# Small loads and stores on GpSimd's queue, a margin in the order of TensorE's work, and longer lines for the cache products

## The chip, the cores and the metric

The kernel runs on one core of one Trainium2 chip. The metric is device time in microseconds (us) of one launch, the median over runs. TensorE (PE in the profile; PEld is its weight load), VectorE (DVE), ScalarE (ACT), GpSimd (POOL) and SyncE (SP) each run their own instruction stream in order. Transfers between HBM and SBUF are issued from an engine's queue, and 16 DMA engines carry them.

## The reference

One layer of a hybrid decoder in float32, for 512 prompt tokens and for 8 sample tokens that have 4096 cached positions each:

```python
z = rmsnorm(x) @ w_in                      # 1024 -> 3584
o_hg, s_hg = hgrn2_recurrence(...)         # gated linear recurrence, 4 heads
o_da = attend(q_da, k_da, v_da, lam)       # differential attention, 4 heads, 2 maps each
x = x + concat(o_hg, o_da) @ w_out
x = x + cross_attn(rmsnorm(x), mk, mv)     # 256 memory tokens
x = x + swiglu(rmsnorm(x), w_gate, w_up, w_down)   # 1024 -> 2816 -> 1024
y = rmsnorm(x)
```

For the sample tokens the attention reads 8 x 32 pages of 128 positions of a key cache and as many of a value cache (67 MB each), found through a page table, and the recurrence makes one step from a stored state for each of the 8 requests. Outputs are y, the new states, and the new keys and values of both parts and of the memory.

## The kernel before

**Weights.** All weights are read once as a planned list of 512 KB pieces (`load_weights`, SP's queue, ring of 3 `raw` buffers). Each half piece (128x512, a "weight tile") is split by ACT (`hi`) and DVE (`lo`), and a product of the prompt is three matmuls on such splits. `done["used"]` counts the weight tiles consumed: w_in is 0 to 56, the memory's keys and values 56 to 88, w_out, w_mq and w_mo 88 to 136, and the feed-forward weights the rest.

**Cache.** Key pages and value pages come as 512 KB buffers (2 pages) of a ring of 6, also over SP's queue. `score_keys` consumes 128 such buffers in lumps of 4 (64 matmuls into `ks`); `sum_values` consumes 128 more (matmuls into `pv`). `pace` gives these streams a high rank as long as they are behind a straight line over the weight tiles, and a rank behind the prompt's products when they are ahead of it: `KPACE = (10, 62)` is the line for the keys, `VPACE = (60, 136)` that for the values.

**The sample recurrence** (`sample_recurrence`, once for the prompt's recurrence heads are under way): `svq` is written to a scratch in DRAM (`spill`, tile `vd`); then for each of 8 requests the state `st` (256 KB) is loaded, and `kv`, one row of `vd` spread over all 128 partitions in runs of 512 bytes (`load_row`, 256 KB). ACT multiplies `kv` by the key column, DVE updates `st`, `st` is stored as `hg_sample`, and TensorE forms `so` from it.

**The order of work** is written by a planner that runs while the program is built. `Clock` keeps an estimate of when each engine, tile and transfer is free; `note` adds each instruction as it is emitted. Every piece of work is a generator (a stream) with a rank. It yields a tuple of tiles ("when these are ready"), nothing ("when what I just issued is done"), a time, or a condition. `Weave.run` walks the streams by rank and lets the first go on whose time is not later than TensorE's estimated free time; if there is none, the one with the earliest time. The engines execute in the order in which the planner emitted, and wait on semaphores where the estimate was too early. The estimate for a transfer on SP's queue is: it begins 1.1 us after issue, moves 0.39 MB per us behind the transfers before it, and is known 0.93 us after its end.

All transfers but the load of the parameters and half of the final stores are on SP's queue.

Of the kernel before, what the change touches and what calls it, by code (L numbers as in the profile page):

```python
# [20 lines left out]
P = 128  # L21
# [12 lines left out]
LAM_INIT = 0.2  # L34
LEVELS = (16, 8, 4, 2, 1)
BIG = 1e37
SLOTS = 62
SCRATCH = 4
RAW = 3
HILO = 3  # L40
KPG = 2
KBUFS = 6
LUMP = 4
KPACE = (10, 62)
VPACE = (60, 136)
NEAR, FAR = 2, 4
PBATCH = 8
LEAD = 10.0
# [84 lines left out]
class Clock:  # L133
# [99 lines left out]
    def note(self, e, op, ins):  # L233
        i = ins.ins
        outs = [y.bass_ap for y in i.outs if hasattr(y, "bass_ap")]
        srcs = [y.bass_ap for y in i.ins if hasattr(y, "bass_ap")]
        mine = lambda aps: [a.tensor.name for a in aps if self.tc.is_my_tile(a.tensor)]
        ws, rs = mine(outs), mine(srcs)
        start = self.free[e]
        at = "dma" if op == "dma_start" else e  # L240
        for t in ws + rs:
            w, by = self.wrote.get(t, (0.0, ""))
            if by != at or at == "dma" and t in rs:
                start = max(start, w + self.LATE.get(by, 0.0))
        for t in ws if at != "dma" else ():
            start = max(start, self.used.get(t, 0.0))
        if op == "dma_start":
            start = max(start, self.free["issue"])
            self.free["issue"] = start + 0.56
            self.free[e] = start + (0.56 if e == "sp" else 0.06)  # L250
            begin = max(self.free["dma"], start + 1.1)
            a = outs[0] if ws else srcs[0]
            end = self.free["dma"] = begin + 4 * int(np.prod(a.shape)) / 0.39e6
            done = end + 0.93
            e = "dma"
        else:
            aps = outs + (srcs if e != "pe" else [])
            n = max(int(np.prod(a.shape[1:])) for a in aps)
            holds = self.shared(e, op, outs, srcs)
            if holds:  # L260
                for a, b in self.port["pool" if e == "dve" else "dve"]:
                    if a <= start < b:
                        start = b
            done = end = start + self._cost(e, op, outs[0].shape, [a.dtype for a in outs + srcs], n)
            if e == "pe":
                form = "narrow" if outs[0].shape[0] < P else "wide" if F32R in [a.dtype for a in srcs] else "exact"
                done = end = end + CHANGE.get((self.form, form), 0.0)
                self.form = form
                self.records += 2 if form == "wide" or op == "transpose" else 4
                if self.records >= 256:  # L270
                    self.records -= 256
                    done = end = self.fetched = max(end, self.fetched + FETCH)
                tick, rows = int(start / TICK), srcs[0].shape[0] / P
                if self.columns.get(tick - 1, 0) < FULL:
                    done = end = end + (end - start)
                self.columns[tick] = self.columns.get(tick, 0) + n * rows * (1 if F32R in [a.dtype for a in srcs] or op == "transpose" else 2)
            self.free[e] = end
            self.span = (start, end)
            if holds:
                self.port[e].append((start, end))  # L280
        for t in ws:
            self.wrote[t] = (done, e)
            self.mark = max(self.mark, done + self.LATE.get(e, 0.0))
        self.noted += 1
        for t in ws + rs:
            self.used[t] = max(self.used.get(t, 0.0), end)
            if t in self.banks:
                self.banks[t][1] = self.noted
# [19 lines left out]
class Weave:  # L308
# [8 lines left out]
        self.clock, self.streams = clock, []  # L317

    def add(self, gen, rank, uses=""):
        self.streams.append([rank, 0.0, None, gen, uses])  # L320

    @staticmethod
    def rank(s):
# [13 lines left out]
    def run(self):  # L337
        c = self.clock
        while self.streams:
            now = c.free["pe"]  # L340
            self.streams.sort(key=self.rank)
            best, when = None, 0.0
            for s in self.streams:
                if s[2] is not None:
                    if not s[2]():
                        continue
                    s[2] = None
                t = self._time(s)
                if best is None or t < when:
                    best, when = s, t  # L350
                if t <= now:
                    break
            assert best is not None, "every stream waits"
            c.mark = 0.0
            try:
                y = next(best[3])
            except StopIteration:
                self.streams.remove(best)
                continue
            if y is None:  # L360
                best[1] = c.mark
            elif callable(y):
                best[1], best[2] = 0.0, y
            elif isinstance(y, tuple):
                best[1] = c.ready(y)
            else:
                best[1] = y
# [3 lines left out]
def decode_step(ctx: ExitStack, tc: tile.TileContext, io: dict):  # L371
# [6 lines left out]
    pool = clock.engine("pool", real.gpsimd)  # L378
    sync = clock.engine("sp", real.sync)
# [5 lines left out]
    sp = ctx.enter_context(tc.tile_pool(name="sp", bufs=2))  # L385
# [175 lines left out]
    def spill(q, name):  # L561

        d = dp.tile([P, P], F32, name=name)
        sync.dma_start(d, q)
        return d.rearrange("(g b) c -> b g c", b=32)

    def load_row(dst, d, b):

        sync.dma_start(dst.rearrange("p (g c) -> p g c", g=4), d[b].partition_broadcast(P))


    sizes = [512] * (DFF // 512)
# [162 lines left out]
    S = {}  # L735
# [104 lines left out]
    def evac_qk(which):  # L840
        def f(t, acc):
            z = slot("z")
            act.activation(z, acc, AF.Copy, scale=rtok[:, t : t + 1])
            return rotate(t, z)

        def rotate(t, z):
            yield (z,)
            yield from room()
            o = slot("ro")
            rope_tok(v3(z), ropep[:, t, :], v3(o))  # L850
            yield (o,)
            if which == "k":
                sync.dma_start(io["k_prompt"][t * P : (t + 1) * P, :], o)
            yield from at_room()
            pt = att("qkt")
            for h in range(HEADS):
                tr(pt[:, h * P : (h + 1) * P], o[:, h * P : (h + 1) * P], ident)
            yield (pt,)
            if which == "q":
                qT[t] = slot("qT")  # L860
                act.copy(qT[t], pt)
                give(1)
            else:
                for h in range(HEADS):
                    if kT[h] is None:
                        kT[h] = slot("kT")
                    act.copy(kT[h][:, t * P : (t + 1) * P], pt[:, h * P : (h + 1) * P])
                give(2)
                done["k"] += 1
            at_give()  # L870

        return f
# [6 lines left out]

    def store(dst, t):  # L880
        yield (t,)
        sync.dma_start(dst, t)

    def s_rope(acc, scale, name, read=None):
        z = quadt("sz", tag="fq", bufs=3)
# [97 lines left out]
    def score_keys():  # L983

        yield lambda: "qst" in S
        for n in range(0, NB * nst, LUMP):
# [4 lines left out]
            yield lambda: n + LUMP - 1 in kts  # L991
            yield (*(kts[n + i] for i in range(LUMP)), *qst)
            cols = slice(s % 4 * P, (s % 4 + 1) * P)
            for y in range(2):
                for b in range(b0, b0 + LUMP):
                    for g in range(4):
                        h = 2 * (g % 2) + y
                        mm(
                            acc[32 * g : 32 * g + 32, cols],
                            qst[b // 4][:, b % 4, h, :],  # L1000
                            kts[n + b - b0][:, g // 2, h * P : (h + 1) * P],
                            b + y == 0,
                            b + y == NB,
                        )
# [301 lines left out]
    def hg_head(h):  # L1306
# [104 lines left out]
            )  # L1411
        at_give()
        yield
        sync.dma_start(io["hg_prompt"][h], st[:, 3 * P :])
        yield from at_room()
        out = att("ohg")
        for c in range(NT):
# [48 lines left out]
    def sample_recurrence(sqT, sfT, svq, sgT):  # L1466
# [14 lines left out]
        yield from room(2)  # L1481
        for b in range(NB):
            st = slot("st")
            sync.dma_start(st, io["state"][b])
            kv = slot("kv")
            load_row(kv, vd, b)
            yield
# [14 lines left out]
                    st[:, sl], st[:, sl], sfT[:, h, b : b + 1], kv[:, sl], op0=ALU.mult, op1=ALU.add  # L1502
                )
            yield
            sync.dma_start(io["hg_sample"][b], st)
            yield from at_room()
            po = att("so")
            for h in range(HEADS):
# [79 lines left out]
    def evac_mk(half):  # L1588
# [4 lines left out]

        def rest(t, o):
            yield (o,)
            sync.dma_start(io["mem_k"][t * P : (t + 1) * P, half * 512 : (half + 1) * 512], o)
            yield from at_room()
            pt = att("mkt")
            for j in range(4):
# [39 lines left out]
    def load_residual():  # L1639
        for j in range(KT):  # L1640
            yield from room()
            xr[j] = slot("res")
            sync.dma_start(xr[j], io["xpT"][j * P : (j + 1) * P, :])
            yield 0.0

    def squares(t, sq):
# [440 lines left out]
    def sample_query(hs):  # L2087
# [16 lines left out]
        yield from s_gemm(hs, 2560, acc[:, :P], KT, width=P)  # L2104
        yield (acc,)
        S["k"] = yield from s_rope(acc[:, :P], 1.0, "ks", at_give)
        sync.dma_start(io["k_sample"], S["k"])
        yield from new_scores()
        S["sn"] = True
        yield lambda: V_FROM in raws  # L2110
# [494 lines left out]
```

## Time and profile before

| | |
|---|---|
| median of 3 runs | 1150.04 us (1149.22 to 1154.39) |
| the profiled execution, its own time | 1160.71 us |
| its span, first to last instruction | 1158.6 us |
| mean granted TensorE clock | 0.974 of full speed |
| busy: PE, PEld, DVE, ACT, POOL | 94%, 68%, 48%, 37%, 3% |
| moved by DMA | 271.38 MB, mean 234 GB/s |

The profiled execution is one run of the program under the hardware profiler; its stages and waits are read by their size against its own time, and the runs without profiler are the metric. A busy PE is not a PE at its peak: the ends of matmuls are modelled. A granted clock of 1.00 in a stretch means 2.4 GHz throughout, and the part that is missing was run at 1.2 GHz.

### The profile page before, as it was taken

What the parts mean: (1) busy time and instruction counts of PE and PEld (TensorE: products, weight loads), DVE (VectorE), ACT (ScalarE), POOL (GpSimd) and SP (SyncE); (2) the same over time, 40 slices, a digit from 0 to 9 for tenths busy, and PEclk for the clock granted to TensorE, in tenths of its full rate; (3) what the DMA queues carried; (4) which work ended last, traced back from release to release, by engine and by line L of the source; (5) the groups of instructions that cost most, each with busy time, mean ns of one, the idle gap of its engine ahead of it and who ended that gap; (6) DMA issues with size and microseconds to landing.
All of it is one profiled execution on the core that took longest, in us unless ns stands there. A gap on an engine that the chain in (4) does not pass through costs nothing.

```text
span 1158.6 us, 23172 instructions
## 1 busy us (share of the span) xinstructions
PE 1092.8 (94%) x8909; PEld 783.3 (68%) x8909; DVE 551.9 (48%) x1128; ACT 427.8 (37%) x910; POOL 38.5 (3%) x42
## 2 busy tenths in 40 slices
PE   8999899978778899999999999999999999999997
PEld 6767677755556544666677766556678788777776
DVE  6741787513655654244355544333334335344545
ACT  5411544313635665233354423223123122222333
POOL 0000010000400000000011000000000000000001
PEclk9999999989888899999999999999999999999998
DMA  7889958878888689999987687999843221233202
GB/s 263 297 296 308 308 197 277 294 256 244 282 257 291 186 300 353 358 366 327 331 264 253 202 309 268 372 366 378 287 154 87 87 83 52 68 109 110 56 1 73
DMA packets 146273, 271.38 MB, mean 234 GB/s; under 512 B 14833, under 2 KB 25073, under 8 KB 146162
## 3 DMA queue, kind: packets, MB, share of 16 engines
q1 hardware_dynamic: 144930, 268.79, 68.1%
q8 instruction: 70, 1.15, 0.4%
q10 hardware_dynamic: 1232, 1.11, 0.3%
q14 instruction: 41, 0.34, 0.1%
HBM read 260.96 MB, written 8.88 MB: 233 GB/s over the span
## 4 chain that ended last, share of the span: by engine, by line
PE 71%; DMA 16%; DVE 5%; SPq 3%; issue 3%; ACT 2%; DVEq 0%; ACTq 0%
PE mm L301 49%; DMA cache_k<-cache_k 6%; PE pv L301 5%; PE ks L301 4%; SPq L301 3%; DMA cache_v<-cache_v 2%; DMA kv<-vd 2%; PE cs L301 2%; PE sdn L301 2%; PE sgu L301 2%; DMA raw<-w_in 1%; PE sgm L301 1%; DMA gu<-w_up 1%; PE co L301 1%; DVE lo L301 1%
## 5 line engine op out<-in xcount | busy, mean ns | idle before, releaser
L301 DVE TENSOR_TENSOR lo<-raw,hi 128x512 fp32r<-128x512 f32 (+1 forms) x260 | 177.5, 684 | 414.2 <-ACT hi L301 362.9
L301 PE MATMUL mm<-sh,hi 128*128 128x512 f32 (+1 forms) x832 | 339.3, 408 | 0.3 <-ACT hi L301 0.3
L301 ACT CAST hi<-raw 128x512 fp32r<-128x512 f32 (+1 forms) x260 | 157.3, 606 | 460.0 <-PE mm L301 407.1
L301 PE MATMUL mm<-sl,hi 128*128 128x512 f32 (+1 forms) x832 | 323.9, 389 | 0.6 <-DVE sl L301 0.6
L301 PE MATMUL mm<-sh,lo 128*128 128x512 f32 (+1 forms) x832 | 323.1, 388 | 0.0
L301 PEld LDWEIGHTS mm<-sh,hi 128*128 128x128 f32 x832 | 157.5, 189 | 73.5 <-issue 39.0
L301 PEld LDWEIGHTS mm<-sh,lo 128*128 128x128 f32 x832 | 157.6, 189 | 33.7 <-DVE lo L301 0.4
L301 PEld LDWEIGHTS mm<-sl,hi 128*128 128x128 f32 x832 | 158.0, 190 | 28.4 <-DVE sl L301 1.0
L301 PE MATMUL ks<-cache_k,qst 128*32 128x128 f32 x2048 | 78.3, 289 | 9.1 <-DMA cache_k<-cache_k 7.7
L301 PEld LDWEIGHTS ks<-cache_k,qst 128*32 128x32 f32 x2048 | 59.8, 115 | 29.8 <-DMA cache_k<-cache_k 19.9
L301 PE MATMUL pv<-cache_v,wt 128*32 128x512 f32 x512 | 67.6, 599 | 1.2 <-DMA cache_v<-cache_v 1.2
L301 PE MATMUL mm<-hi,sh 128*128 128x512 f32 x128 | 56.2, 439 | 0.0
L301 PE MATMUL mm<-lo,sh 128*128 128x512 f32 x128 | 51.3, 401 | 0.0
L301 PE MATMUL mm<-hi,sl 128*128 128x512 f32 x128 | 51.2, 400 | 0.0
L301 DVE TENSOR_TENSOR res<-mm,res 128x512 f32<-128x512 f32 (+1 forms) x68 | 42.4, 654 | 11.4 <-PE mm L301 11.3
L301 PEld LDWEIGHTS pv<-cache_v,wt 128*32 128x32 f32 x512 | 15.2, 109 | 36.4 <-issue 22.5
L301 PEld LDWEIGHTS mm<-hi,sh 128*128 128x128 f32 x128 | 24.9, 195 | 7.9 <-issue 3.4
L301 PE MATMUL mm<-hi,mh 128*128 128x512 f32 x64 | 29.7, 464 | 0.0
L301 PEld LDWEIGHTS mm<-hi,sl 128*128 128x128 f32 x128 | 24.8, 194 | 5.8
L301 PEld LDWEIGHTS mm<-lo,sh 128*128 128x128 f32 x128 | 25.1, 196 | 4.5 <-issue 0.5
L301 PE MATMUL mm<-lo,mh 128*128 128x512 f32 x64 | 25.5, 399 | 0.0
L301 PE MATMUL mm<-hi,ml 128*128 128x512 f32 x64 | 25.5, 398 | 0.0
(410 smaller groups left out, 1170.3 us busy)
## 6 DMA issues: line engine op xcount, KB each, us to landing
cache_k<-cache_k SPq DMA_DIRECT2D x256, 256.0 KB, 5.5
cache_v<-cache_v SPq DMA_DIRECT2D x256, 256.0 KB, 5.0
raw<-w_in SPq DMA_DIRECT2D x27, 512.0 KB, 5.7
raw<-w_down SPq DMA_DIRECT2D x22, 512.0 KB, 3.8
raw<-w_gate SPq DMA_DIRECT2D x20, 512.0 KB, 4.1
raw<-w_up SPq DMA_DIRECT2D x20, 512.0 KB, 3.8
cache_mem_k<-cache_mem_k SPq DMA_DIRECT2D x16, 512.0 KB, 7.4
cache_mem_v<-cache_mem_v SPq DMA_DIRECT2D x16, 512.0 KB, 7.2
```

What stands on the lines that cost most here:

```text
L301: ins = getattr(self.engine, op)(*a, **k)
```

## The change

1. Transfers that are stores or small loads go from SP's queue to GpSimd's: `spill` (1), `load_row` (8), the stores of the prompt's keys (4) and values (4), of the sample's key and value (2), of the prompt's states (4), of the memory's keys (4) and values (4), the loads (8) and stores (8) of the sample's states, and the loads of the residual (8): 55 transfers. Weights, cache pages, x and the last stores stay where they were.
2. The planner's estimate for a transfer on GpSimd's queue: the queue is held 1.0 us, the transfer begins 2.0 us after issue. All transfers are estimated at 0.37 in place of 0.39 MB per us.
3. After a stream yielded a tuple of tiles or nothing, it counts as ready for the walk by rank only when TensorE's estimated time is `MARGIN = 1.0` us past its own. If no stream is ready with its margin, the one with the earliest time goes on, without a margin.
4. `KPACE` goes from (10, 62) to (10, 80), `VPACE` from (60, 136) to (80, 150), `SLOTS` from 62 to 63.
5. In `score_keys` the loop over the 4 buffers of a lump is put outside the loop over the two maps.

```diff
-SLOTS = 62
+SLOTS = 63
-KPACE = (10, 62)
-VPACE = (60, 136)
+MARGIN = 1.0
+KPACE = (10, 80)
+VPACE = (80, 150)
@@ Clock.note
         if op == "dma_start":
-            start = max(start, self.free["issue"])
-            self.free["issue"] = start + 0.56
-            self.free[e] = start + (0.56 if e == "sp" else 0.06)
-            begin = max(self.free["dma"], start + 1.1)
+            if e == "pool":
+                self.free[e] = start + 1.0
+            else:
+                start = max(start, self.free["issue"])
+                self.free["issue"] = start + 0.56
+                self.free[e] = start + (0.56 if e == "sp" else 0.06)
+            begin = max(self.free["dma"], start + (1.1 if e != "pool" else 2.0))
             a = outs[0] if ws else srcs[0]
-            end = self.free["dma"] = begin + 4 * int(np.prod(a.shape)) / 0.39e6
+            end = self.free["dma"] = begin + 4 * int(np.prod(a.shape)) / 0.37e6
@@ Weave.run
-                if t <= now:
+                if t + s[5] <= now:
+                    best = s
                     break
...
             c.mark = 0.0
+            best[5] = 0.0
...
+            if y is None or isinstance(y, tuple):
+                best[5] = MARGIN
@@ spill, load_row, evac_qk, store, hg_head, sample_recurrence, evac_mk, load_residual, sample_query
-        sync.dma_start(d, q)
+        pool.dma_start(d, q)
...
-        sync.dma_start(dst.rearrange("p (g c) -> p g c", g=4), d[b].partition_broadcast(P))
+        pool.dma_start(dst.rearrange("p (g c) -> p g c", g=4), d[b].partition_broadcast(P))
...
@@ score_keys
-            for y in range(2):
-                for b in range(b0, b0 + LUMP):
+            for b in range(b0, b0 + LUMP):
+                for y in range(2):
```

## Rows read from the trace of the kernel before

**Rows 1.** The page: span, and busy time of each engine.
```profile
span 1158.6 us, 23172 instructions
PE 1092.8 (94%) x8909; PEld 783.3 (68%) x8909; DVE 551.9 (48%) x1128; ACT 427.8 (37%) x910; POOL 38.5 (3%) x42
```
**Rows 2.** By stage: us, busy time of each engine, granted clock, DMA share, GB/s.
```profile
0.00:230.00 230.00, 213.62 (x3168) 165.94 (x3169) 139.28 (x312) 91.89 (x200) 8.98 (x15) 0.97 0.82 279
230.00:410.00 180.00, 146.97 (x1360) 103.59 (x1359) 88.58 (x229) 82.26 (x208) 12.34 (x9) 0.89 0.78 248
410.00:460.00 50.00, 45.44 (x280) 24.04 (x279) 24.85 (x58) 31.39 (x73) 0.00 (x0) 1.00 0.98 349
460.00:685.00 225.00, 225.00 (x1239) 148.42 (x1241) 95.71 (x168) 87.80 (x181) 11.30 (x10) 1.00 0.87 301
685.00:850.00 165.00, 163.67 (x1084) 103.57 (x1077) 64.10 (x129) 46.55 (x88) 0.62 (x2) 1.00 0.86 320
850.00:1096.00 246.00, 244.14 (x1507) 191.53 (x1506) 106.12 (x176) 67.59 (x124) 0.00 (x0) 1.00 0.30 90
1096.00:1158.60 62.60, 53.98 (x284) 46.20 (x282) 33.26 (x59) 20.32 (x38) 5.31 (x6) 0.95 0.11 35
```
**Rows 3.** Waits of all engines: engine, for what, us in total, times, longest.
```profile
ACT kv L301 <- DMA kv<-vd: 39.1, 7, 12.8
```
**Rows 4.** Timeline, PE and one row of ACT, 236 to 396: start, us, idle before it.
```profile
252.53 1.41 PE L301 MATMUL so<-st,qm 128*32 128x128 f32 x8 [5.76 <-issue]
...
267.42 1.28 PE L301 MATMUL so<-st,qm 128*32 128x128 f32 x8 [1.60 <-DVE st L301]
...
346.00 1.28 ACT L301 ACTIVATE kv<-kv,skT 128x128 f32<-128x128 f32 x4 [7.30 <-DMA kv<-vd]
...
347.67 0.79 PE L301 MATMUL sc<-kT,qT 64*128 64x128 f32 x2 [6.34 <-ACT pr L301]
...
371.49 1.12 PE L301 MATMUL mkt<-con,mk 128*128 128x128 f32 x4 [3.54 <-ACT mk L301]
...
395.87 1.65 PE L301 MATMUL oda<-pr,vda 128*128 128x128 f32 x6 [2.77 <-ACT pr L301]
```
**Rows 5.** The chain that ended last, in order of time: start, us, what.
```profile
258.96 1.88 PE ks L301 x64
...
348.46 3.57 PE ks L301 x64
```
**Rows 6.** Cache pages: idle before their products (us, times), the products, PE's own idle.
```profile
  DMA cache_k<-cache_k: 27.6, 57
...
  DMA cache_v<-cache_v: 14.3, 29
...
L301 PE MATMUL ks<-cache_k,qst x2048: 272/273/423, 51.7 to 376.8; 128*32 128x128 f32 x187
...
L301 PE MATMUL pv<-cache_v,wt x512: 592/592/617, 407.1 to 685.5; 128*32 128x512 f32 x171
...
L301 PE MATMUL ks<-cache_k,qst 128*32 128x128 f32 x2048 | 78.3, 289 | 9.1 <-DMA cache_k<-cache_k 7.7
...
L301 PE MATMUL pv<-cache_v,wt 128*32 128x512 f32 x512 | 67.6, 599 | 1.2 <-DMA cache_v<-cache_v 1.2
```
**Rows 7.** DMA issues: KB each, median us from issue to landing.
```profile
st<-state SPq DMA_DIRECT2D x8, 256.0 KB, 5.3
kv<-vd SPq DMA_DIRECT2D x8, 256.0 KB, 10.1
```
**Rows 8.** Waits of SP's queue, 230 to 300 and 300 to 420.
```profile
SPq L301 <- DMA vd<-svq: 4.1, 1, 4.1
...
SPq L301 <- DVE st L301: 9.5, 2, 9.1
```
**Rows 9.** POOL's costliest group, and DVE's (min/median/max ns).
```profile
L301 POOL TENSOR_TENSOR res<-sh,sl 128x512 f32<-128x512 f32 x8 | 10.5, 1342 | 287.5 <-ACT cp L301 281.1 <-PE co L301 6.4
...
L301 DVE TENSOR_TENSOR lo<-raw,hi x260: 422/692/1776, 5.9 to 1139.2; 128x512 fp32r<-128x512 f32 x122, 128x256 fp32r<-128x256 f32 x8
```

More of the change, by code (lines that the diff above doesn't have):

```diff
@@ L319, in add @@
     def add(self, gen, rank, uses=""):
-        self.streams.append([rank, 0.0, None, gen, uses])
+        self.streams.append([rank, 0.0, None, gen, uses, 0.0])
     @staticmethod
@@ L852, in rotate @@
             if which == "k":
-                sync.dma_start(io["k_prompt"][t * P : (t + 1) * P, :], o)
+                pool.dma_start(io["k_prompt"][t * P : (t + 1) * P, :], o)
             yield from at_room()
@@ L881, in store @@
         yield (t,)
-        sync.dma_start(dst, t)
+        pool.dma_start(dst, t)
     def s_rope(acc, scale, name, read=None):
@@ L1413, in hg_head @@
         yield
-        sync.dma_start(io["hg_prompt"][h], st[:, 3 * P :])
+        pool.dma_start(io["hg_prompt"][h], st[:, 3 * P :])
         yield from at_room()
@@ L1483, in sample_recurrence @@
             st = slot("st")
-            sync.dma_start(st, io["state"][b])
+            pool.dma_start(st, io["state"][b])
             kv = slot("kv")
@@ L1504, in sample_recurrence @@
             yield
-            sync.dma_start(io["hg_sample"][b], st)
+            pool.dma_start(io["hg_sample"][b], st)
             yield from at_room()
@@ L1595, in rest @@
             yield (o,)
-            sync.dma_start(io["mem_k"][t * P : (t + 1) * P, half * 512 : (half + 1) * 512], o)
+            pool.dma_start(io["mem_k"][t * P : (t + 1) * P, half * 512 : (half + 1) * 512], o)
             yield from at_room()
@@ L1642, in load_residual @@
             xr[j] = slot("res")
-            sync.dma_start(xr[j], io["xpT"][j * P : (j + 1) * P, :])
+            pool.dma_start(xr[j], io["xpT"][j * P : (j + 1) * P, :])
             yield 0.0
@@ L2106, in sample_query @@
         S["k"] = yield from s_rope(acc[:, :P], 1.0, "ks", at_give)
-        sync.dma_start(io["k_sample"], S["k"])
+        pool.dma_start(io["k_sample"], S["k"])
         yield from new_scores()
```

## Prediction

> **What bounds the kernel now.** I read the page first: TensorE is busy 94% of the span [rows 1], so a change that removes no product can win only what TensorE loses: its idle time and the time at the lower clock. The view by stages says where these lie [rows 2]. Up to 460 us TensorE idles 16.4 + 33.0 + 4.6 = 54.0 us; after that, 0 + 1.3 + 1.9 + 8.6 = 11.8 us, most of it in the last 63 us, which no part of the change touches. The granted clock is 0.97, 0.89 and 1.00 in the first three stages. A clock of 0.89 over 180 us costs 0.11 x 180 = 19.8 us of full-speed work, 0.97 over 230 us costs 6.9 us. So some 81 us are to be had before 460 us, and 53 of them in the 180 us from 230 to 410. The DMA engines are not full there (share 0.78), though they are from 410 to 460 (0.98 at 349 GB/s).
>
> What stalls TensorE between 230 and 410? The waits of the engines [rows 3] show ACT standing 39.1 us in 7 waits for the load of kv. ACT works in order, so the splits of weights and the softmax pieces emitted behind that multiply stand as well. The timeline shows the stalls that follow: 5.76 and 1.60 us before so, 6.34 before a score, 3.54 before a transpose, 2.77 before an attention product, together 20.0 us; the third ends 1.7 us after a kv wait of 7.30 us [rows 4]. The chain of waits then shows what a stall does to the clock [rows 5]: 64 key products take 1.88 us at full speed and 3.57 us right after the 6.34 us stall, the lower of the two levels (1.2 against 2.4 GHz). Kv takes so long because of its shape: it lands 10.1 us after issue, the state load of the same size 5.3 us [rows 7], while the planner reckons 1.1 + 0.67 + 0.93 = 2.7 us when the DMA queue is free.
>
> The second loss is spread out: before products on cache pages TensorE or its weight load sat 27.6 us in 57 waits for keys and 14.3 us in 29 waits for values; TensorE's own idle of it is 7.7 + 1.2 = 8.9 us [rows 6]. The third is SP's queue: in the stage of the recurrence it stood 9.5 us for a store that waited for DVE, and 4.1 us for the spill to land before kv could be issued [rows 8], with cache pages and weights queued behind.
>
> **The change, part by part.**
>
> *kv and its margin.* By the new estimate kv is due 2.0 + 0.71 + 0.93 = 3.64 us after issue, and the stream that yielded nothing gets 1.0 us more while others have work. ACT's multiply is therefore ordered 4.64 - 2.70 = 1.94 us later against the rest. If kv lands as late as now, 7 waits of 5.6 us on average shorten by 1.94 each: 13.6 of 39.1 us, or 35%. What hangs on these waits is 20.0 us of stalls and the stage's 19.8 us of clock, 39.8 us, about 1.0 us of TensorE per us of ACT's wait. The term is 0.35 x 39.8 = 13.9 us. Bounds: no row shows a transfer on GpSimd's queue. If kv lands like the state load, at 5.3 us, the waits vanish (5.3 - 4.64 is under 1 us) and the term is 39.8 us. If its shape costs as much again (10.1 - 5.3 = 4.8 us), it lands at 14.9 us and 8 loads lose 8 x 4.8 = 38 us. I take 10.1, the only row of this shape.
>
> *Margin, slower transfers, pace and loop order, for the cache products.* The mean wait there is 41.9 / 86 = 0.49 us, under the margin of 1.0. A 256 KB page is estimated 0.04 us longer, a lump of 8 pages 0.3 us. With the loop turned round the last buffer of a lump is first needed after 24 products, not 12: at 1.88 / 64 = 0.029 us each that is 0.35 us later. The key pace now spreads the last (80 - 62) / 70 = 26% of 67 MB, some 17 MB or 49 us of transfer at 349 GB/s, behind weight tile 62; the values follow by 14 tiles. That relieves the stages before 410 us and loads those from 410 to 850, where the DMA share is already 0.98 to 0.86 and TensorE has no idle time to lose it in. Nothing in all this moves more bytes per second, so part of what a product no longer waits for is waited for elsewhere. Bounds: 0, if all of it is, and 41.9 us. I take the row nearest to TensorE's own loss, 8.9 us.
>
> *SP's queue.* 9.5 + 4.1 = 13.6 us of standing go. What was late behind it were pages and weights; in this stage TensorE idles 33.0 of 180 us (18%), in the rest it had other work. 0.18 x 13.6 = 2.5 us; bounds 0 and 13.6. The store, and the next state load behind it, now stand on POOL's queue in the same order. What else is queued there is the gating of the recurrence heads, which w_out needs only from 460 us on, and later the residual's sums.
>
> *What GpSimd pays.* POOL is busy 38.5 us of 1158.6 [rows 1]. Even at the length of its longest common instruction, 1.342 us [rows 9], 55 issues are 74 us in an engine that idles 97% of the time: 0 on the path. SP sheds 55 issues; 0 too, since it waits for buffers anyway. The slot more is 0, nothing waits for slots in the rows read.
>
> *Later sample work.* The values end at tile 150 instead of 136. They took 278 us for the 76 tiles of their old line [rows 6], 3.7 us a tile, so the sample's remaining path starts some 51 us later. It moves into the stages from 685 to 1096, where TensorE is busy throughout and the DMA share falls to 0.30 [rows 2]: 0, covered by the feed-forward products, and up to 51 us if that path became the last to end.
>
> Sum: 13.9 + 8.9 + 2.5 = 25.3 us. The profiled execution would go from 1160.7 to 1135.4 us. It lies 10.7 us over the median of the runs, so I take the same 25 us from the median: 1150 - 25 = 1125 us.
>
> **A rule that speaks against it.** SP's queue, on which kv comes now, is held up by waits alone [rows 8]; no engine that computes takes part in it. The Trainium skill, "SBUF — State Buffer", section "SBUF: two separate sides", says that descriptors of transfers issued from GpSimd are written by GpSimd itself, which cannot write them while DVE holds their shared SBUF port in certain modes; its example goes from about 620 ns to about 3100 ns. By that example, an estimate, 8 loads of kv would lose 8 x 2.5 = 20 us, and the sum would be 5 us in place of 25. No row here shows a transfer on that queue, so the trace can't say yet.
>
> **Rivals.**
>
> *Slower: kv late on the new queue.* Its 512 runs are prepared by an engine that shares work time with DVE, which is busy 88.6 of 180 us in this stage [rows 2] in pieces of 0.69 us, up to 1.78 [rows 9]. Each us of later landing costs 8 us on ACT and, by the ratio above, 8 us on TensorE, so 25 / 8 = 3.1 us per load eat the gain, and the 4.8 us of the bound give 1125 + 38 = 1163 us. Against it: POOL is idle and its instructions finish beside DVE at 1.3 us.
>
> *More: kv quick on its own queue.* Now kv stands behind the pages issued before it on SP's queue. If a queue of its own lands it near 5.3 us, the first term is 39.8 instead of 13.9: 1125 - 26 = 1099 us. Against it: the state load stands on the same queue and needs half the time, so most of the 10.1 is the shape.
>
> *Nothing: the waits move.* The planner's order is as wrong as before elsewhere, the pages that come later stall the values from 410 to 850, where rows show the DMA engines full, and only SP's 2.5 us remain: 1147 us. For it: bytes and products are the same. Against it: the clock stage has its own cause, kv.
>
> **How the numbers follow.** Forecast (1110 to 1140): 0.48. More: 0.16. Nothing: 0.16. Slower: 0.20. A measurement of this kernel can tell about 0.5%, 5.8 us, from no change. Forecast and "more" are faster, with a sliver of "nothing" (0.01): 0.65. Same: 0.15. Slower: 0.20. The range goes from 1097, the "more" case, to 1158, which takes in "nothing" and the mild half of "slower"; outside it are about 0.06 below and 0.12 above.
>
> **What would show it.** Right: ACT's wait for kv falls from 39.1 to about 25 us; TensorE's idle time between the start of the recurrence and the end of the keys falls by some 10 us or more and the clock there rises over 0.92; the waits before cache products go well under 41.9 us; the keys end near weight tile 80 and the stages after that stay without idle time. Kv's landing decides between the cases: about 10 us for the forecast, 5 to 7 for more, 13 and over for slower. Wrong: ACT's kv waits as long or longer, POOL's transfers late, TensorE idle between 410 and 850 us, or the last stage waiting for the sample's path.

## The result, and the profile after

The changed kernel takes 1141.7 us (median of 6, 1134.9 to 1143.8) against 1152.2 us for the kernel before in the same comparison (1149.2 to 1157.5): ratio 0.9891, 95% interval 0.9849 to 0.9934. That is 10.5 us faster, where 25 us were forecast. The time lies inside the range and the direction holds; the gain is less than half of the forecast.

The two profiled executions differ by more than the medians: 1160.7 us before, 8.5 over its median, and 1134.9 after, 6.9 under its own. Of the 25.9 us between them 15.4 are not in the medians. The stages of the changed kernel, from its page and the view by stages (columns as in [rows 2]):

```profile
span 1133.1 us, 23098 instructions
...
PE 1072.3 (95%) x8846; PEld 777.3 (69%) x8846; DVE 546.1 (48%) x1126; ACT 428.3 (38%) x915; POOL 70.4 (6%) x97
...
0.00:230.00 230.00, 213.91 (x3025) 170.84 (x3026) 141.24 (x323) 93.42 (x207) 18.28 (x32) 0.96 0.77 255
230.00:410.00 180.00, 149.92 (x1468) 106.14 (x1470) 94.73 (x230) 90.27 (x224) 28.46 (x35) 0.92 0.96 284
410.00:460.00 50.00, 48.46 (x352) 34.51 (x341) 23.30 (x62) 30.20 (x68) 6.01 (x12) 0.98 0.71 238
460.00:685.00 225.00, 222.18 (x1248) 144.88 (x1249) 99.14 (x175) 88.24 (x180) 11.29 (x10) 0.99 0.91 311
```

Against [rows 2], the bad stage is still there: from 230 to 410 us TensorE idles 30.1 us (33.0 before) and the clock is 0.92 (0.89). The view of the waits says that its old cause has shrunk, ACT's waits for kv from 39.1 us [rows 3] to this:

```profile
ACT kv L305 <- DMA kv<-vd: 21.1, 3, 9.3
```

and the views of the cache pages' tiles say what came instead (idle before the products; key products first and last start; landing; then the values):

```profile
  DMA cache_k<-cache_k: 40.0, 36
...
L305 PE MATMUL ks<-cache_k,qst x2048: 272/273/423, 47.5 to 418.8; 128*32 128x128 f32 x187
...
DMA to landing us min/median/max: 2.7/5.6/15.4
...
  DMA cache_v<-cache_v: 8.3, 24
```

The waits for values fell from 14.3 to 8.3 us, those for keys rose from 27.6 to 40.0 [rows 6], in fewer and longer pieces. The key stage ends at 419 us instead of 377. TensorE's own waits from 230 to 410 us show the exchange, before and after: what it loses to the softmax and the recurrence shrinks, what it loses to key pages grows from 5.9 to 16.0 us.

```profile
PE sc L301 <- ACT pr L301: 6.3, 1, 6.3
PE ks L301 <- DMA cache_k<-cache_k: 5.9, 11, 2.1
PE so L301 <- issue: 5.8, 1, 5.8
```
```profile
PE ks L305 <- DMA cache_k<-cache_k: 16.0, 10, 6.0
PE sc L305 <- ACT pr L305: 4.9, 1, 4.9
PE so L305 <- issue: 3.6, 1, 3.6
```

The timeline of TensorE has the longest such wait, and the chain of waits what it waited for: a key page that was 13.7 us on its way; the store of a state, the load of a state and a kv were issued 0.9 to 2.0 us after it.

```profile
265.04 1.53 PE L305 MATMUL ks<-cache_k,qst 128*32 128x128 f32 x16 [5.99 <-DMA cache_k<-cache_k]
```
```profile
251.28 13.71 DMA cache_k<-cache_k
265.04 1.53 PE ks L305 x16
```

On GpSimd's queue kv lands after 11.4 us (10.1 before, [rows 7]), and an issue costs POOL 0.55 us, or 0.76 us for kv. The load of a quarter of the memory, which is still on SP's queue, lands after 12.5 us, where it took 9.4 before (DMA issues, then POOL's groups):

```profile
mt<-memT SPq DMA_DIRECT2D x4, 256.0 KB, 12.5
...
st<-state POOLq DMA_DIRECT2D x8, 256.0 KB, 6.1
kv<-vd POOLq DMA_DIRECT2D x8, 256.0 KB, 11.4
```
```profile
L305 POOL DMA_DIRECT2D kv<-vd x8 | 6.1, 758 | 5.4 <-DMA vd<-svq 5.4
...
L305 POOL DMA_DIRECT2D out_hg_sample<-st x8 | 4.4, 550 | 126.3 <-DVE st L305 78.4 <-DVE pz L305 22.8 <-DMA cache_k<-cache_k 14.5
```

### The profile page after: what moved, and what is told of

The parts are those of the page before. It is cut to its first block, busy times and chain, and to the rows that moved or that the text cites. A ratio compares the mean times of both kernels' runs of the same rounds, so it can differ in the third digit from the quotient of the medians.

```text
span 1133.1 us, 23098 instructions
## 1 busy us (share of the span) xinstructions
PE 1072.3 (95%) x8846; PEld 777.3 (69%) x8846; DVE 546.1 (48%) x1126; ACT 428.3 (38%) x915; POOL 70.4 (6%) x97
## 2 busy tenths in 40 slices
DMA packets 143376, 279.75 MB, mean 247 GB/s; under 512 B 15281, under 2 KB 20529, under 8 KB 143266
## 3 DMA queue, kind: packets, MB, share of 16 engines
q0 software_dynamic: 4064, 13.05, 6.1%
## 4 chain that ended last, share of the span: by engine, by line
PE 81%; DMA 10%; DVE 3%; issue 3%; ACT 1%; SPq 1%; POOL 0%; DVEq 0%; POOLq 0%; ACTq 0%
PE mm L305 56%; DMA cache_k<-cache_k 6%; PE pv L305 5%; PE ks L305 4%; PE sgu L305 2%; PE cs L305 2%; PE sdn L305 1%; DMA kv<-vd 1%; PE ss L305 1%; PE co L305 1%; PE sgm L305 1%; PE pd L305 1%; PE sacc L305 1%; PE oda L305 1%; PE cpv L305 1%
## 5 line engine op out<-in xcount | busy, mean ns | idle before, releaser
L305 PE MATMUL ks<-cache_k,qst 128*32 128x128 f32 x2048 | 72.3, 285 | 16.1 <-DMA cache_k<-cache_k 16.0
L305 PE MATMUL pv<-cache_v,wt 128*32 128x512 f32 x512 | 63.4, 608 | 0.0
L305 DVE SCALAR_TENSOR_TENSOR lo<-raw,par,hi 128x512 fp32r<-128x512 f32 x16 | 13.2, 826 | 35.1 <-ACT hi L305 35.1
L305 PE MATMUL mm<-hi,mh 128*128 128x512 f32 x64 | 28.5, 446 | 0.9 <-ACT hi L305 0.9
```

Of the source, the lines that this page charges most:

```text
L305: ins = getattr(self.engine, op)(*a, **k)
```

## The experiments

The kernel before had medians of 1149.1 to 1152.2 us in the comparisons below; each ratio is against it.

| kernel | median us | ratio, 95% interval |
|---|---|---|
| changed | 1141.7 | 0.989 (0.985 to 0.993) |
| e1 queue alone | 1167.1 | 1.015 (1.013 to 1.017) |
| e2 margin alone | 1142.9 | 0.992 (0.990 to 0.995) |
| e3 paces alone | 1150.5 | 1.001 (0.999 to 1.003) |
| e4 changed, kv a plain load | 1096.1 | 0.953 (0.951 to 0.955) |
| e5 changed, no margin | 1143.1 | 0.993 (0.989 to 0.996) |
| e6 changed, old paces | 1122.3 | 0.975 (0.972 to 0.978) |
| e7 changed, SP's queue | 1138.1 | 0.988 (0.983 to 0.993) |
| e8 changed, kv in 2 KB runs | 1098.2 | 0.955 (0.951 to 0.960) |
| e9 as e8, old paces | 1098.4 | 0.953 (0.950 to 0.957) |
| e10 as e8, no margin | 1112.8 | 0.966 (0.963 to 0.969) |
| e11 as e8, SP's queue | 1099.8 | 0.955 (0.952 to 0.959) |
| e12 before, kv in 2 KB runs | 1121.7 | 0.973 (0.969 to 0.976) |
| e13 changed, old key line | 1121.0 | 0.976 (0.972 to 0.979) |
| e14 changed, old value line | 1137.1 | 0.989 (0.986 to 0.991) |
| e15 changed, lines half way | 1148.2 | 0.999 (0.997 to 1.001) |
| e16 as e8, margin 2.0 | 1101.8 | 0.957 (0.955 to 0.960) |

**One part alone.** e1 takes part 1, in all ten calls, and of part 2 the estimate for GpSimd's queue:

```diff
-        sync.dma_start(d, q)
+        pool.dma_start(d, q)
...
+            if e == "pool":
+                self.free[e] = start + 1.0
```

> The kernel before with the 55 transfers on GpSimd's queue and their estimate alone; no margin, old paces, old loop order, 62 slots, 0.39 MB per us. Theory order (the gain is the margin's: it orders ACT's multiply by kv later): within 4 us of before, ACT's waits for kv still above 30 us. Theory queue (the gain is SP's queue freed of stores and spill): 6 to 12 us faster. Theory paces: within 4 us.

It is 18 us slower, so neither theory foresaw it. ACT's waits for kv nearly vanish, yet cache pages are late by far more (waits of the engines, then idle before key and value products):

```profile
ACT kv L305 <- DMA kv<-vd: 6.5, 2, 5.3
```
```profile
  DMA cache_k<-cache_k: 62.1, 63
...
  DMA cache_v<-cache_v: 36.3, 40
```

e2 takes part 3 alone:

```diff
+MARGIN = 1.0
...
-                if t <= now:
+                if t + s[5] <= now:
+                    best = s
                     break
```

> The kernel before with the margin of 1.0 us alone, all transfers on SP's queue. Theory order: 6 to 12 us faster, ACT's waits for kv about 30 us. Theory queue: within 4 us. Theory paces: within 4 us.

It is 6 us faster at the medians, as theory order said, but not for its reason: ACT's waits for kv stay at 41.1 us (39.1 before), while the waits before key products go from 27.6 to 21.6.

e3 takes the two lines of part 4 alone:

```diff
-KPACE = (10, 62)
-VPACE = (60, 136)
+KPACE = (10, 80)
+VPACE = (80, 150)
```

> The kernel before with the two longer lines for keys and values alone. Theory paces (fewer pages early relieve the first 410 us): 6 to 12 us faster, waits before cache products under 30 us. Theories order and queue: within 4 us, the waits only move.

No difference. The three parts add to a loss of some 13 us, and the change is a gain of 10. Either the parts do not add, or what was not run alone (loop order, 0.37, the slot) makes up 24 us; the next runs speak for the first.

**What kv does to the pages beside it.** e4 and e8 change one load of the changed kernel; e4 first.

```diff
-        pool.dma_start(dst.rearrange("p (g c) -> p g c", g=4), d[b].partition_broadcast(P))
+        pool.dma_start(dst, io["state"][b])
```

> The changed kernel in which each kv is loaded as a plain 256 KB state (128 rows of 2 KB) in place of one row spread over all partitions in runs of 512 bytes, so that the sample's recurrence is computed from other numbers; size, queue and order are the same. Theory shape (kv's pattern holds up the cache pages in flight beside it, which is where the gain went): kv lands in 5 to 7 us, the 40.0 us of waits before key products fall under 25, and the kernel is 8 to 20 us faster than the changed one. Theory full engines (the pages are late because the DMA engines are full then): kv lands at 9 us or later, the key waits stay above 33 us, and the time stays within 4 us of the changed kernel's.

And e8:

```diff
-        d = dp.tile([P, P], F32, name=name)
-        pool.dma_start(d, q)
-        return d.rearrange("(g b) c -> b g c", b=32)
+        d = dp.tile([32, T], F32, name=name)
+        for g in range(4):
+            pool.dma_start(d[:, g * P : (g + 1) * P], q[32 * g : 32 * g + 32, :])
+        return d
...
-        pool.dma_start(dst.rearrange("p (g c) -> p g c", g=4), d[b].partition_broadcast(P))
+        pool.dma_start(dst, d[b].partition_broadcast(P))
```

> The changed kernel with the scratch in DRAM written so that the row of a request lies in one piece of 2 KB (4 small transfers in place of one); each kv is then still one row spread over 128 partitions, but in 128 runs of 2 KB in place of 512 of 512 bytes. Theory runs (the number of short runs costs the time): kv lands in 5 to 8 us, the kernel is 20 to 45 us faster than the changed one. Theory one place (all 16 DMA engines read the same 2 KB of HBM, whatever the length of the runs): kv lands at 9 us or later and the time stays within 6 us of the changed kernel's.

They are 46 and 44 us faster than the changed kernel, and e8 does all its work. For e4 that is over twice what theory shape expected; its signs, kv's landing and the waits before key products, came as it said. The stage from 230 to 410, kv's landing, and the idle time before key products, first e4, then e8:

```profile
230.00:410.00 180.00, 172.85 (x1726) 126.24 (x1719) 111.99 (x275) 113.66 (x277) 30.12 (x44) 0.98 0.90 320
...
kv<-state POOLq DMA_DIRECT2D x8, 256.0 KB, 6.2
...
  DMA cache_k<-cache_k: 11.4, 22
```
```profile
230.00:410.00 180.00, 173.58 (x1739) 127.77 (x1741) 113.00 (x283) 113.94 (x278) 33.39 (x47) 0.99 0.92 323
...
kv<-vd POOLq DMA_DIRECT2D x8, 256.0 KB, 7.2
...
  DMA cache_k<-cache_k: 13.4, 25
```

TensorE idles 6.4 us in that stage in place of 30.1, the clock is 0.99 in place of 0.92, and the same DMA engines move 323 GB/s in place of 284, at a share of 0.92 in place of 0.96. So they were not full of bytes before: they were busy with kv. The page's line for GpSimd's queue shows it directly, the changed kernel first, then e8 (packets, MB, share of the 16 engines' span):

```profile
q0 software_dynamic: 4064, 13.05, 6.1%
```
```profile
q0 software_dynamic: 4160, 13.05, 3.4%
```

The same 13.05 MB took the 16 engines 6.1% of 1133.1 = 69 us and 3.4% of 1097.0 = 37 us, so the eight slow loads held all of them for 32 us more, 4.0 us each. Theory full engines falls, and so does theory one place, as 128 reads of one 2 KB row are quick. Whether it is the number of runs (512 against 128) or that a request's four pieces lay 16 KB apart in the scratch, the runs don't separate.

**The changed kernel with one part taken back.** e5 sets `MARGIN = 0.0`, e6 the two old lines, e7 puts `sync` for `pool` in all ten calls.

> The changed kernel with the margin set to 0. The queue alone made the kernel 18 us slower than before and the margin alone 7 us faster. Theory sum (the parts add): about 1149 us, 7 to 8 us over the changed kernel. Theory pair (the margin mends the damage of the queue's move, so without it the changed kernel falls back further): 1158 us or more, ACT's waits for kv above 30 us.

> The changed kernel with the old paces (10, 62) and (60, 136). Theory sum: within 4 us of the changed kernel, as the paces alone did nothing. Theory pair (the longer lines matter only beside the other parts, where more pages are in flight beside the slow kv): 6 us slower or more, waits before key products over 40 us.

> The changed kernel with all transfers back on SP's queue; margin, paces, loop order, slot and 0.37 stay. Theory sum: the queue's move costs 18 us, so this gives about 1124 us. Theory pair (the move pays once the margin orders the waits): 1141 us or slower.

Without the margin the changed kernel is 1.4 us slower, inside the scatter: neither theory. ACT's waits for kv are then 6.6 us, less than the 21.1 with it. On SP's queue it is 3.6 us faster at the medians, inside the scatter: under the 1141 of theory pair, but far from the 1124 of theory sum, as the 18 us of e1 are not there. ACT waits longer for kv in it than in the kernel before (39.1 us):

```profile
ACT kv L305 <- DMA kv<-vd: 48.5, 7, 9.8
```

The large one is e6: the longer lines cost 19 us here, though alone they cost nothing. Neither theory foresaw that sign. ACT waits 3.9 us for kv and key products 34.1 (waits; then the stage; then the tile):

```profile
ACT kv L305 <- DMA kv<-vd: 3.9, 4, 1.6
...
230.00:410.00 180.00, 161.77 (x1486) 117.08 (x1474) 103.32 (x266) 99.06 (x253) 29.99 (x39) 0.94 0.95 278
...
  DMA cache_k<-cache_k: 34.1, 37
```

**Which line, and is it steady?** e13 and e14 put back one line each, e15 sets (10, 71) and (70, 143).

> The changed kernel with the old line for the keys (10, 62) and the new one for the values. Theory overlap (longer key loading keeps pages in flight beside all eight slow kv loads): 1119 to 1127 us, as with both old lines. Theory values (the values' line costs it): 1138 us or more.

> The changed kernel with the old line for the values (60, 136) and the new one for the keys. Theory overlap: within 5 us of the changed kernel's 1142. Theory values: 1119 to 1127 us.

> The changed kernel with both lines half way, (10, 71) and (70, 143). Theory overlap: half way between, 1128 to 1136 us. Theory accident of order (small shifts decide what stands behind a slow kv): outside 1120 to 1143, or at one of the two ends within 3 us.

The keys' line costs nearly all of it: 1121.0 with the old one, while the old line for the values gives 1137.1, near the changed kernel's 1141.7. But half way is slower than either end, at 1148.2, with 28.5 us of ACT's waits for kv and 59.7 us before key products. So it does not grow with the line: theory overlap holds for which line, and theory accident for how much.

**The parts again, with a quick kv.**

> The changed kernel with kv in runs of 2 KB and with the old paces. In the changed kernel the new paces cost 19 us. Theory kv (they cost it because more of the key stage runs beside the slow kv): with the quick kv the difference shrinks, 1092 to 1104 us against 1098 with the new paces. Theory paces (the longer lines are bad by themselves): 1086 us or less.

> The changed kernel with kv in runs of 2 KB and the margin set to 0. Theory margin (products wait for results whose time is estimated too early, everywhere): 1104 us or more against 1098. Theory kv (what the margin did for the kernel before was to wait less behind kv): within 4 us of 1098.

> The changed kernel with kv in runs of 2 KB and all transfers back on SP's queue. Theory queue (stores that wait at the head of SP's queue hold up pages whatever kv does): 1104 us or more against 1098. Theory kv: within 4 us.

> The kernel before with nothing changed but kv in runs of 2 KB (and its scratch written in 4 pieces). Theory kv: 30 us or more faster than before, 1120 us or less, ACT's waits for kv under 12 us. Theory parts (the gain of the quick kv needs the margin and the queue): 1130 us or more.

> The changed kernel with kv in runs of 2 KB and a margin of 2.0 us. A margin of 1.0 gave 14.7 us with the quick kv. Theory more (estimates are off by more than 1 us in many places): 1092 us or less. Theory enough (1.0 covers the usual error): within 4 us of 1098.

Old paces 1098.4 and SP's queue 1099.8 against 1098.2: with a quick kv, and beside the margin, both parts are worth nothing that can be told from 0. The margin is worth 14.7 us (e10), so it does mend waits elsewhere: theory margin, not theory kv. The view of the waits shows some of the places, e10 first and e8 second (TensorE's own waits for DVE and the pauses of its weight load that no view puts down to another engine):

```profile
PE kdt L305 <- DVE zf L305: 5.0, 3, 2.5
PE pt L305 <- DVE pr L305: 4.0, 6, 1.6
...
PEld mm L305 <- issue: 56.1, 143, 0.8
```
```profile
PE kdt L305 <- DVE zf L305: 2.2, 1, 2.2
...
PE pt L305 <- DVE pr L305: 0.5, 1, 0.5
...
PEld mm L305 <- issue: 46.0, 114, 1.4
```

A margin of 2.0 gives 1101.8, no more than 1.0 does. The kernel before with nothing but the quick kv takes 1121.7 us, 29.7 under before, between the two theories (1120 and 1130); its stage from 230 to 410 idles 10.4 us:

```profile
ACT kv L301 <- DMA kv<-vd: 6.4, 4, 2.7
...
230.00:410.00 180.00, 169.56 (x1571) 113.47 (x1570) 106.94 (x281) 107.59 (x272) 11.27 (x9) 0.99 0.90 315
```

## Why the prediction was right in direction and wrong in size

**Where the loss lies** was right. The quick kv alone recovers 29.7 us of the kernel before, and the quick kv with the change 54: the stage and the load at its root were named.

**The premise** that the change can win only idle time and lost clock, with products and bytes the same, did not hold. Between the two profiled executions TensorE's idle time fell from 65.8 to 60.8 us and the mean clock is 0.974 in both, but its busy time fell from 1092.8 to 1072.3. The new order takes more of the sample's later weights from loads of their own: 8909 products became 8846, and 271.38 MB became 279.75. The products concerned took 7 us less; the other 13 of the 20.5 are no more than the 15.4 by which the two executions differ beyond the medians. In time it shows nothing: with the quick kv 8909 products (e9) take as long as 8846 (e8).

**The kv term (13.9 us)** had the right landing (11.4 us, close to the 10.1 taken) and a fall of ACT's waits (18.0 us) not far from the 13.6 reckoned, but not its reason and not its price. The reason was to be the later order, by the margin above all. The margin alone leaves ACT's waits at 41.1 us (e2), and with margin and SP's queue they are 48.5 (e7); with GpSimd's queue and no margin they are 6.5 and 6.6 (e1, e5). So they fell with the move to GpSimd's queue, of which the new estimate is a part; the margin did not lower them, and that 18.0 lies near 13.6 is luck. The price was "about 1.0 us of TensorE per us of ACT's wait". In e1 ACT's waits fall by 32.6 us, and TensorE idles as long in the stage as before:

```profile
230.00:410.00 180.00, 147.56 (x1362) 101.32 (x1355) 88.43 (x234) 87.17 (x218) 24.92 (x32) 0.91 0.87 250
...
PE ks L305 <- DMA cache_k<-cache_k: 22.3, 14, 5.8
```

What the term left out is the second victim, the pages in flight beside kv, which landed up to 15.4 us after issue (12.3 before). Idle time and lost clock of the stage fell by 2.9 + (19.8 - 14.4) = 8.3 us. The prediction counted kv's slowness only where ACT waits for it, not in what the DMA engines can't carry meanwhile. The two waits beside each other (us; idle is TensorE's from 230 to 410):

| kernel | ACT for kv | before key products | idle | median |
|---|---|---|---|---|
| before | 39.1 | 27.6 | 33.0 | 1152.2 |
| e1 queue alone | 6.5 | 62.1 | 32.4 | 1167.1 |
| changed | 21.1 | 40.0 | 30.1 | 1141.7 |
| e7 changed, SP's queue | 48.5 | 32.9 | 32.6 | 1138.1 |
| e15 lines half way | 28.5 | 59.7 | 30.7 | 1148.2 |
| e6 changed, old paces | 3.9 | 34.1 | 18.2 | 1122.3 |
| e12 before, 2 KB runs | 6.4 | 22.5 | 10.4 | 1121.7 |
| e8 changed, 2 KB runs | 8.1 | 13.4 | 6.4 | 1098.2 |

ACT's column alone does not tell the time; where both waits are small, the stage's idle time is small too. From before to changed the two add to 66.7 and 61.1 us: most of what ACT no longer waited for was waited for before key products. That is the rival "the waits move", at work inside the kv term, and within the stage of the keys rather than in that of the values.

**The cache term (8.9 us)** is the step that failed. Its text allowed that "part of what a product no longer waits for is waited for elsewhere", but set the bounds at 0 and 41.9 us and said that the new line "relieves the stages before 410 us". Measured, the waits before cache products rose from 41.9 to 48.3 us: the keys' by 12.4, while the values' fell by 6.0. TensorE's own idle time of it, the 8.9 us that the term took as a gain, became 16.0:

```profile
L305 PE MATMUL ks<-cache_k,qst 128*32 128x128 f32 x2048 | 72.3, 285 | 16.1 <-DMA cache_k<-cache_k 16.0
```

The longer lines cost 19.4 us beside the slow kv (e6), nearly all of it the keys' line (e13). The bound below 0 was missing. With the old lines the change gives 29.6 us, close to the 25 forecast. That is luck too: without the cache term the sum is 16.4, and the margin, on which the first two terms rest, is worth 14.7 us under a quick kv (e10) and 1.4 us in the changed kernel (e5).

**SP's queue (2.5 us)**: e7 and e11 find nothing that can be told from 0. So the waits at the head of SP's queue cost nothing that these runs can tell. That fits what the Trainium skill says in "DMA: Bandwidth & Descriptors", section "Issuing engines are not separate DMA queues": all queues end on the same 16 DMA engines, and issuing from several saves only the time of issue. The two pairs of runs agree; the 18 us lost in e1 show that the move of transfers can still cost.

**What GpSimd pays**: nothing speaks against the 0. POOL's busy time went from 38.5 to 70.4 us, in an engine that idles 94% of the time, and with the transfers back on SP's queue (e7) the time is the same within the scatter.

**The rule on descriptors** from "SBUF — State Buffer" of the Trainium skill, which made the rival of a late kv, shows nothing of its 2.5 us a load here: with all other parts the same kv lands after 11.6 us on SP's queue (e7) and 11.4 on GpSimd's, beside a DVE that is busy 53% of the stage. The quick kv lands after 6.1 us on SP's queue (e11) and 7.2 on GpSimd's (e8), 1.1 us later. Whether DVE's operations here run in the modes that the rule is about, no run shows. The DMA issues of e7:

```profile
kv<-vd SPq DMA_DIRECT2D x8, 256.0 KB, 11.6
```

**The base.** Taking 25 us from the median was sound, but the profiled execution of before was 8.5 us over its median, so the stalls read from it were those of an execution slower than most.

**What stays open.** Why the keys' line costs 19 us beside the slow kv and half of its shift costs 26 is shown only as far as this: it needs the slow kv (e9), it is the keys' line (e13), and it is not steady (e15). That each order happens to put other work beside the eight slow loads fits all of it and was not shown load by load. For the 18 us of e1 the views show late pages, not why they are later than in e6. One part of it may be that the slow kv is dearer on GpSimd's queue: it held the 16 engines 32 us longer than the quick one there, but only some 16 us on SP's queue (71.2% of 1138.0 us in e7 against 72.6% of 1093.8 in e11, at the same bytes). That alone does not explain it, as e6 pays it too: GpSimd's queue took 5.5% of 1164.1 = 64 us in e1 and 5.6% of 1122.1 = 63 us in e6. Loop order, 0.37 and the slot were not run alone; with a quick kv they stand between e12 and e10, 8.8 us, next to the queue and the lines, which are worth nothing beside the margin.

## What to carry to other kernels

A transfer that takes twice the time of its equals at the same size can be a loss in two places: in the engine that waits for it and in the transfers beside it, so mend its pattern before the order around it. Here one row of 2 KB in one piece was worth 30 us in the kernel before and 44 in the changed one, where the whole change was worth 10. When parts of a change reorder work around such a load, measure each with and without the others and with the load mended, as their signs can turn. And a bound for "the waits may move" must reach below zero.

## What the runs showed of the hardware that was not expected

A 256 KB load that spreads a row over 128 partitions lands after 10.1 to 12.5 us when the row is four runs of 512 bytes 16 KB apart, and after 5.4 us (e12, SP's queue) to 7.3 us (e10, GpSimd's) when it is one run of 2 KB. In the stage of the slow loads the DMA engines showed a share of 0.96 and moved 284 GB/s; with the quick ones 0.92 and 323 GB/s. Eight slow loads of 256 KB held all 16 engines 32 us longer than eight quick ones on GpSimd's queue, and some 16 us longer on SP's. A busy share is not a measure of bytes.
